# Hybrid backbone on one core: layer norms with centerings first and squares on GpSimd, bias tables two heads at a time

## Chip, cores and metric

The kernel runs on one core of a Trainium2 chip. The metric is the device time of one execution in microseconds (us), the median of the runs. Engines are named as in the profile: PE is TensorE, PEld its weight loads, DVE VectorE, ACT ScalarE, POOL GpSimd, SP the queue of SyncE that issues most of the DMAs.

## What is computed

Two layers over 512 latent and 256 context tokens of width 1024. A layer is a half-step SwiGLU feed-forward network (FFN, inner width 2816), a token mixer, and a second FFN; every sub-layer is modulated by the conditioning vectors and closed by a layer norm.

```python
def layer_norm(x, g, b):
    mu = jnp.mean(xf, axis=-1, keepdims=True)
    var = jnp.mean(jnp.square(xf - mu), axis=-1, keepdims=True)
    return ((xf - mu) * lax.rsqrt(var + LN_EPS)).astype(x.dtype) * g + b

def swiglu(u, w_in, w_out):
    a, v = jnp.split(u @ w_in, 2, axis=-1)
    return (jax.nn.silu(a) * v) @ w_out

def ffn_sublayer(h, shift, scale, gate, w_in, w_out, g, b):
    y = swiglu(modulate(h, shift, scale), w_in, w_out)      # h * (1 + scale) + shift
    return layer_norm(ALPHA * h + FFN_RES * gate * y, g, b)
```

Mixer 0 is a neighbourhood attention (8 x 16 windows on the token grid, 16 heads, a learned bias per head) over latent and context keys; mixer 1 is a windowed attention with grouped keys (band of 128 tokens on each side) over latent and context keys. The shift, scale and gate vectors are products of the conditioning vectors with a large modulation matrix.

## The kernel before

**Layout.** Activations are held transposed: eight tiles `z` of 128 features by all tokens (one of them at times in `zspare`), and their modulated form as a pair of high and low parts, `uh` and `ul`. Weights come as raw tiles `wr` by the SP queue (L94), and are split into `wh` on ACT (L102) and `wl` on POOL (L104), so each product is three matmuls (L153 to L155).

**Stages.** FFN 0a, neighbourhood attention (NA), FFN 0b, FFN 1a, windowed attention (WA), FFN 1b. An FFN runs over chunks 0 to 10 of its inner width and once more over a part of the tokens ("r"). In the middle chunks `seven` (L590) forms two 2x2 block products with seven instead of eight multiplications from sums of token and weight blocks; `sums` and `fourth` (L518 to L559) make the token sums, `fourth` in chunk 1 for the chunks behind. `av` (L465) makes the gated product g as `gh` and `gl` (L478 to L481), and `down` multiplies it by the output weights and adds the result to z on DVE (L453).

**Background products.** `gemv_dve` (L195) computes part of the modulation vectors on DVE while TensorE does an FFN: each product multiplies a tile `wt` (L205, 256 KB by the SP queue) with a broadcast row and sums it into `ga` (L208); the results are then added up and derived into scale and bias of a layer norm (L229, L230, L254 to L262). A pace spreads the products over the chunks; in the last chunks they run thinly, one behind each piece of `av` and `down`.

**Layer norms.** `layer_norm` gives four parts, which are called at points of the program by a table (`plan`, the agenda): `sums` adds the eight z tiles (four on POOL, the rest on DVE), `centers` forms the mean with one matmul and then, tile by tile, subtracts it on DVE (L347), squares on ACT (L419) and adds up the squares (L331), `variance` and `spreading` end in the factor by which `norm` multiplies z (L438). Tiles for squares come from a pool of two (tag "ln"). l0 to l4 are the norms between the stages, `l1_0` that of the first token group behind NA, `l4_0` that of the first group behind WA, `fin_0` and `fin_1` the last ones. `fin_1` sums its squares on TensorE (`layer_norm_pe`).

**Order.** The program is written in one sequence, and the framework's scheduler sets the order of each engine's queue from it; `behind(x, y)` keeps x behind y on one engine. So an edit of the agenda moves rows on all engines.

**Bias tables.** `bias_tables` reads the bias of NA into a scratch tensor `xd` (eight DMAs) and spreads it into `yd`, one DMA of 252 KB for each of 16 heads (L826). NA reads `yd` later into `nb`.

## Time and profile before

| | |
|---|---|
| three timed runs | 2860.63 us median (2854.68, 2860.63, 2862.81) |
| profiled execution | 2868.23 us, span 2866.4 us |
| mean granted clock of PE | 0.972 of full speed |
| busy, PE / PEld | 2728.1 us (95%) / 2447.8 us (85%) |
| busy, DVE / ACT / POOL | 1805.4 us (63%) / 1213.4 us (42%) / 1658.0 us (58%) |
| instructions | 48106 |

A row of a timeline reads: start in us, length in us, engine, line, operation, output <- inputs, shape, count of rows that were merged, and in brackets the idle time of that engine before it and what ended it. PE is busy in 95% of the span, so its waits and its stretches at half clock are what can be read as lost time.

### The profile page before, as it was taken

What the parts mean: (1) busy time and instruction counts of PE and PEld (TensorE: products, weight loads), DVE (VectorE), ACT (ScalarE), POOL (GpSimd) and SP (SyncE); (2) the same over time, 40 slices, a digit from 0 to 9 for tenths busy, and PEclk for the clock granted to TensorE, in tenths of its full rate; (3) what the DMA queues carried; (4) which work ended last, traced back from release to release, by engine and by line L of the source; (5) the groups of instructions that cost most, each with busy time, mean ns of one, the idle gap of its engine ahead of it and who ended that gap; (6) DMA issues with size and microseconds to landing.
All of it is one profiled execution on the core that took longest, in us unless ns stands there. A gap on an engine that the chain in (4) does not pass through costs nothing.

```text
span 2866.4 us, 48106 instructions
## 1 busy us (share of the span) xinstructions
PE 2728.1 (95%) x17122; PEld 2447.8 (85%) x17122; DVE 1805.4 (63%) x4124; ACT 1213.4 (42%) x2497; POOL 1658.0 (58%) x1488
## 2 busy tenths in 40 slices
PE   8999999999999989999999999999998998899997
PEld 5789899888888878999998899998886776888997
DVE  3286777585545676766654776666566667687744
ACT  4223333256454444434333534343246555444443
POOL 4357575375434455876744677765466444577763
PEclk9999999999999989999999999999999999899998
DMA  8525557432212212345462326466522111235562
GB/s 300 141 87 158 133 144 208 134 103 82 60 49 62 58 56 86 97 121 140 119 167 83 96 83 166 134 183 180 174 81 62 31 31 45 59 89 129 123 181 65
DMA packets 286016, 322.42 MB, mean 112 GB/s; under 512 B 28497, under 2 KB 174033, under 8 KB 284753
## 3 DMA queue, kind: packets, MB, share of 16 engines
q1 hardware_dynamic: 269936, 290.89, 34.2%
q0 software_dynamic: 15552, 28.32, 5.9%
q8 instruction: 135, 2.21, 0.3%
q14 instruction: 105, 0.85, 0.1%
q10 hardware_dynamic: 288, 0.14, 0.0%
HBM read 311.41 MB, written 12.25 MB: 113 GB/s over the span
## 4 chain that ended last, share of the span: by engine, by line
PE 52%; DVE 6%; DMA 2%; issue 2%; ACT 1%; POOL 1%; SPq 0%; DVEq 0%; POOLq 0%; ACTq 0%
PE pd1a L153 2%; PE pd0b L153 2%; PE pd1a L154 2%; PE pd0b L154 2%; PE pd0b L155 2%; PE pd1a L155 2%; PE wo L800 1%; PE pd1b L153 1%; PE pd1b L154 1%; PE pd1b L155 1%; DMA wr<-in_wst_dram 1%; PE tpw L791 1%; PE pa1a L153 1%; PE pa1a L154 1%; PE pv1a L153 1%
## 5 line engine op out<-in xcount | busy, mean ns | idle before, releaser
L104 POOL TENSOR_TENSOR wl<-wr,wh 128x512 fp32r<-128x512 f32 x308 | 404.0, 1328 | 298.4 <-ACT wh L102 238.4
L104 POOL TENSOR_TENSOR wl_s<-S,wh_s 128x512 fp32r<-128x512 f32 x202 | 268.4, 1366 | 60.5 <-ACT wh_s L102 59.7
L102 ACT CAST wh<-wr 128x512 fp32r<-128x512 f32 x308 | 186.7, 619 | 215.1 <-DMA wr<-in_wst_dram 62.2
L102 ACT CAST wh_s<-S 128x512 fp32r<-128x512 f32 x216 | 130.9, 620 | 322.4 <-POOL S L574 84.1
L208 DVE CUSTOM_DVE_ANT_0 jk<-wt,cb 128x512 f32<-128x512 f32 x303 | 200.4, 680 | 61.4 <-DMA wt<-in_wmodt_dram 52.1
L574 POOL TENSOR_TENSOR S<-wr,wr 128x512 f32<-128x512 f32 x108 | 146.9, 1360 | 148.6 <-DMA wr<-in_wst_dram 130.1
L104 POOL TENSOR_TENSOR wl_a<-wr,wh_a 128x512 fp32r<-128x512 f32 x120 | 159.1, 1376 | 24.9 <-ACT wh_a L102 24.5
L102 ACT CAST wh_a<-wr 128x512 fp32r<-128x512 f32 x162 | 100.4, 621 | 125.9 <-PE pd1b L154 18.3
L453 DVE SCALAR_TENSOR_TENSOR z<-pd0b,gt,z 128x256 f32<-128x256 f32 (+1 forms) x176 | 103.4, 602 | 62.2 <-PE pd0b L155 62.0
L453 DVE SCALAR_TENSOR_TENSOR z<-pd1a,gt,z 128x512 f32<-128x512 f32 (+1 forms) x168 | 99.8, 619 | 44.5 <-PE pd1a L155 43.3
L807 POOL TENSOR_SCALAR p<-p,l 128x512 f32<-128x512 f32 x64 | 44.6, 698 | 128.9 <-DVE l L906 120.5
L453 DVE SCALAR_TENSOR_TENSOR z<-pd0a,gt,z 128x512 f32<-128x512 f32 (+1 forms) x168 | 98.7, 618 | 29.5 <-PE pd0a L155 28.9
L319 POOL TENSOR_SCALAR z<-z,ag_None,ab_None 128x256 f32<-128x256 f32 (+1 forms) x78 | 63.5, 819 | 53.4 <-DVE uh L305 42.8
L208 DVE CUSTOM_DVE_ANT_0 jk<-zspare,cb 128x512 f32<-128x512 f32 x113 | 75.8, 679 | 15.6 <-DMA zspare<-in_wmodt_dram 15.6
L807 POOL TENSOR_SCALAR pw<-pw,l 128x512 f32<-128x512 f32 (+1 forms) x64 | 41.2, 645 | 74.4 <-DVE l L1097 33.0
L574 POOL TENSOR_TENSOR S<-S,wr 128x512 f32<-128x512 f32 x54 | 77.1, 1427 | 3.2 <-DVE x1b L557 0.7
L574 POOL TENSOR_TENSOR S<-wr,S 128x512 f32<-128x512 f32 x54 | 76.8, 1422 | 2.9
L905 ACT ACTIVATE p<-s,m 128x512 f32<-128x512 f32 x64 | 44.0, 688 | 77.3 <-DVE m L903 72.3
L453 DVE SCALAR_TENSOR_TENSOR z<-pd1b,gt,z 128x512 f32<-128x512 f32 (+1 forms) x98 | 56.8, 609 | 14.8 <-PE pd1b L155 12.3
L306 DVE TENSOR_TENSOR ul<-ufl,uh 128x256 fp32r<-128x256 f32 (+1 forms) x88 | 63.0, 722 | 2.3 <-ACT ufl L301 1.7
L301 ACT ACTIVATE ufl<-z,bi_None,sc_None 128x256 f32<-128x256 f32 (+1 forms) x86 | 54.7, 654 | 22.2 <-DVE z L438 21.9
L153 PE MATMUL pd0a<-gh0a,wh 128*128 128x512 f32 (+1 forms) x144 | 50.6, 365 | 8.3 <-DVE z L453 8.3
(1463 smaller groups left out, 10687.0 us busy)
## 6 DMA issues: line engine op xcount, KB each, us to landing
wr<-in_wst_dram SPq DMA_DIRECT2D x524, 256.0 KB
...
```

What stands on the lines that cost most here:

```text
L102: nc.scalar.copy(hi[:], src[:])
L104: eng.tensor_tensor(out=lo[:], in0=src[:], in1=hi[:].bitcast(F32), op=ALU.subtract)
L153: nc.tensor.matmul(ps, a[0], b[0], start=first, stop=False)
L154: nc.tensor.matmul(ps, a[0], b[1], start=False, stop=False)
L155: last_pe[0] = nc.tensor.matmul(ps, a[1], b[0], start=False, stop=last)
L208: x = nc.vector.tensor_tensor_reduce(out=junk[:], in0=w[:], in1=cb[st], scale=1.0, scalar=0.0, op0=ALU.mult, op1=ALU.add, accum_out=out[st])
L301: nc.scalar.activation(uf[:, :n], zs, AF.Identity, scale=s1, bias=s2)
L306: return hi, nc.vector.tensor_tensor(out=lo, in0=uv, in1=uo.bitcast(F32), op=ALU.subtract)
L319: nc.gpsimd.tensor_scalar(out=zs, in0=zs, scalar1=prm[2][:, d:d + 1], scalar2=prm[3][:, d:d + 1], op0=ALU.mult, op1=ALU.add)
L453: last[0] = nc.vector.scalar_tensor_tensor(out=zt(d, c0, c1), in0=pd, scalar=gt[:, d, st:st + 1], in1=zt(d, c0, c1), op0=ALU.mult, op1=ALU ...
L574: nc.gpsimd.tensor_tensor(out=t[:], in0=a[:], in1=b[:], op=o)
L807: nc.gpsimd.tensor_scalar(out=p, in0=p, scalar1=r, scalar2=0.0, op0=ALU.mult, op1=ALU.add)
```

## The change

1. `layer_norm` now has five parts: sums, mean, centers, variance, spreading. The mean's matmul is a part of its own, and `centers` issues all eight DVE centerings before the first square. For l1_0 and l4_0 (`pool=True`) the eight squares and the seven adds of them run on POOL; ACT loses eight squares for each, DVE five adds and POOL two. The agenda is set anew: for l1_0 the mean stays at o3_0_2 and the centerings move to o3_0_3; for l4_0 sums, mean and centerings are at wo6_2, wo6_3 and wo7_2.
2. The 16 DMAs into `yd` are issued by `bias_rows(2)`, two behind each `seven` of FFN 0a, and no longer in one row after `xd`.
3. `gemv_dve(0)` takes its ranges in the order (40, 72), (24, 40), and the products of 0a end in chunk 9.
4. In `fourth`, and for the weight splits on DVE in FFN 1b, the DVE rows stand behind the last evacuation of g (`evacuated`).
5. `fin_0`'s norm and output are issued inside `layer_norm_pe("fin_1")`, behind fin_1's last centering.

```diff
-    def layer_norm_pe(nm, c0, c1, tags):
+    def layer_norm_pe(nm, c0, c1, tags, between):
...
-        pv = bank(tags[1], f"pv{nm}")
+        pv, made = bank(tags[1], f"pv{nm}"), []
...
-            zs = center(d, c0, c1, pm)
+            zs = center(d, c0, c1, pm, made)
...
+        between(made[-1])
         ve = tp.tile([P, 4], F32, tag="ve", name=f"ve{nm}", bufs=2)[:, :nj]
...
+        def mean():
+            v["pm"] = v["bk"][:, 0:n]
+            behind(nc.tensor.matmul(v["pm"], onesd[:], v["acc"], start=True, stop=True), last_pe[0])
+
         def centers():
-            pm = v["bk"][:, 0:n]
-            behind(nc.tensor.matmul(pm, onesd[:], v["acc"], start=True, stop=True), last_pe[0])
+            zs = [center(d, c0, c1, v["pm"]) for d in range(DT)]
 
             def square(d, acc):
-                zs = center(d, c0, c1, pm)
                 sq = acc if acc is not None else t2(f"sq{nm}_{d}", "ln")[:, :n]
-                nc.scalar.activation(sq, zs, AF.Square)
+                nc.scalar.activation(sq, zs[d], AF.Square)
                 return sq
 
-            v["acc"] = total(f"aq{nm}", n, square, 3, v["part"])
+            if not pool:
+                v["acc"] = total(f"aq{nm}", n, square, 3, v["part"])
+                return
+            v["acc"] = acc = t2(f"aq{nm}")[:, :n]
+            for d in range(DT):
+                sq = t2(f"sq{nm}_{d}", "ln")[:, :n] if d else acc
+                nc.gpsimd.tensor_tensor(out=sq, in0=zs[d], in1=zs[d], op=ALU.mult)
+                if d:
+                    nc.gpsimd.tensor_tensor(out=acc, in0=acc, in1=sq, op=ALU.add)
...
-            nc.vector.tensor_tensor(out=gl[:, c0:c1], in0=pv[:, :n], in1=gh[:, c0:c1].bitcast(F32), op=ALU.subtract)
+            evacuated[0] = nc.vector.tensor_tensor(out=gl[:, c0:c1], in0=pv[:, :n], in1=gh[:, c0:c1].bitcast(F32), op=ALU.subtract)
...
-                nc.vector.tensor_tensor(out=x, in0=x, in1=y, op=ALU.add)
+                behind(nc.vector.tensor_tensor(out=x, in0=x, in1=y, op=ALU.add), evacuated[0])
...
-        weight = [0] + [1.0] * (s0 - 2) + [0] + [1.0] * (NCH - 2 - s0) + [1.2] * (s0 - 1)
+        weight = [0] + [1.0] * (s0 - 2) + [0] + [1.0] * (NCH - 2 - s0) + [1.2]
...
                     seven(f"{nm}_{ci}_{i}", wpos[0] + i, *gs[i])
+                    if mid is not None:
+                        bias_rows(2)
...
-            thin[0] = bool(bg) and NCH - 2 <= (0 if r else ci) < NCH - 3 + s0
+            thin[0] = bool(bg) and ci == NCH - 2
...
-        for h in range(NH):
-            nc.sync.dma_start(yd[h], xd[h].rearrange("r c e -> r (c e)")[:, None, :].broadcast_to([8, 16, RW * 8]))
+
+    heads = list(range(NH))
+
+    def bias_rows(n):
+
+        for _ in range(min(n, len(heads))):
+            h = heads.pop(0)
+            behind(nc.sync.dma_start(yd[h], xd[h].rearrange("r c e -> r (c e)")[:, None, :].broadcast_to([8, 16, RW * 8])),
+                   loaded[0])
...
-            write(layer_norm_pe("fin_1", c0, c1, ("mm", "s", "mm")))
+            write(1, layer_norm_pe("fin_1", c0, c1, ("mm", "s", "mm"), lambda x: write(0, fin[0], x)))
...
-            write(norm)
+            fin.append(norm)
...
-    gemv_dve(0, (24, 40, (0, 1)), (40, 72, (0, 1)))
+    gemv_dve(0, (40, 72, (0, 1)), (24, 40, (0, 1)))
...
-    plan(pon3_0_0_7=l1[0][:1], o3_0_2=l1[0][1:2], pon2_1_256_7=l1[0][2:3], pon2_2_512_7=l1[0][3:4], o3_1_3=l1[0][4:],
...
+    plan(pon3_0_0_7=l1[0][:1], o3_0_2=l1[0][1:2], o3_0_3=l1[0][2:3], pon2_1_256_7=l1[0][3:4], pon2_2_512_7=l1[0][4:5],
...
-    plan(wo6_3=l4[0][:1], wo7_2=l4[0][1:2], pow3_1_256_2=l4[0][2:3], pow3_1_256_6=l4[0][3:5], pow3_1_256_7=l4[1][:1])
+    plan(wo6_2=l4[0][:1], wo6_3=l4[0][1:2], wo7_2=l4[0][2:3], pow3_1_256_2=l4[0][3:4], pow3_1_256_6=l4[0][4:6],
```

**ACT at the end of NA.** These are rows of ACT's queue; p and l are an attention's weights and their row sums, s the scores, tp a transposed p. Before, the squares of l1_0 stand ahead of the exponentials of p of the third key block:

```order
L741 COPY p_0_2_0_10798<-tp_0_2_0_10802 128x512
L419 ACTIVATE aql_0_0_10837<-z_92 128x256
L419 ACTIVATE sql_0_1_10842<-z_93 128x256
L419 ACTIVATE sql_0_2_10846<-z_94 128x256
L419 ACTIVATE pml_0_10767<-z_95 128x256
L419 ACTIVATE sql_0_4_10852<-z_96 128x256
L419 ACTIVATE sql_0_5_10856<-z_97 128x256
L419 ACTIVATE sql_0_6_10860<-z_98 128x256
L419 ACTIVATE sql_0_7_10865<-z_99 128x256
L905 ACTIVATE p_0_3_0_10878,l_0_3_0_10874<-s_0_3_0_10868,m_0_3_0_10873 128x512
L905 ACTIVATE p_0_3_1_10898,l_0_3_1_10894<-s_0_3_1_10888,m_0_3_1_10893 128x512
```

Now, from the same copy on:

```order
L762 COPY p_0_2_0_10795<-tp_0_2_0_10799 128x512
L933 ACTIVATE p_0_3_0_10844,l_0_3_0_10840<-s_0_3_0_10834,m_0_3_0_10839 128x512
L933 ACTIVATE p_0_3_1_10864,l_0_3_1_10860<-s_0_3_1_10854,m_0_3_1_10859 128x512
L762 COPY p_0_3_0_10844<-tp_0_3_0_10848 128x512
L933 ACTIVATE p_1_2_0_11083,l_1_2_0_11079<-s_1_2_0_11073,m_1_2_0_11078 128x512
```

The eight squares are gone from here, and the two exponentials follow the copy.

**POOL at the same place.** L807, and L828 now, is the scaling of p; L885, and L913 now, adds a mask to a bias tile nb. Before:

```order
L885 TENSOR_TENSOR nb_2_11065<-nmask_sb,nb_2_11065 128x768
L331 TENSOR_TENSOR aql_0_0_10837<-aql_0_0_10837,sql_0_1_10842 128x256
L885 TENSOR_TENSOR nb_2_11070<-nmask_sb,nb_2_11070 128x768
L331 TENSOR_TENSOR aql_0_0_10837<-aql_0_0_10837,sql_0_2_10846 128x256
L807 TENSOR_SCALAR p_0_3_0_10878<-p_0_3_0_10878,l_0_3_0_10874 128x512
L807 TENSOR_SCALAR p_0_3_1_10898<-p_0_3_1_10898,l_0_3_1_10894 128x512
```

Now (L438 is the square, L440 the add):

```order
L828 TENSOR_SCALAR p_0_3_0_10844<-p_0_3_0_10844,l_0_3_0_10840 128x512
L828 TENSOR_SCALAR p_0_3_1_10864<-p_0_3_1_10864,l_0_3_1_10860 128x512
L913 TENSOR_TENSOR nb_2_11062<-nmask_sb,nb_2_11062 128x768
L438 TENSOR_TENSOR aql_0_10890<-z_92 128x256
L913 TENSOR_TENSOR nb_2_11067<-nmask_sb,nb_2_11067 128x768
L438 TENSOR_TENSOR sql_0_1_10892<-z_93 128x256
L438 TENSOR_TENSOR sql_0_2_10895<-z_94 128x256
L440 TENSOR_TENSOR aql_0_10890<-aql_0_10890,sql_0_1_10892 128x256
L440 TENSOR_TENSOR aql_0_10890<-aql_0_10890,sql_0_2_10895 128x256
L438 TENSOR_TENSOR sql_0_3_10898<-z_95 128x256
L438 TENSOR_TENSOR sql_0_4_10901<-z_96 128x256
L828 TENSOR_SCALAR p_1_2_0_11083<-p_1_2_0_11083,l_1_2_0_11079 128x512
```

The scaling of p of the third block stands ahead of the squares, that of the next (p_1_2) behind five squares and two adds.

**DVE in chunk 1 of FFN 1b.** L479 and L481 (L497 and L499 now) evacuate g, L453 (L471 now) adds a down product to z, L557 to L559 (L575 to L577) are the fourth sums, L104 a weight split. Before:

```order
L557 TENSOR_TENSOR x1b_4_27764<-x1b_4_27764,x1b_5_27766 128x256
L544 TENSOR_TENSOR T1b_3l<-x1b_1_27318,T1b_3h 128x256
L104 TENSOR_TENSOR wl_a_27805<-wr_00_27796,wh_a_27804 128x512
L557 TENSOR_TENSOR x1b_4_27771<-x1b_4_27771,x1b_5_27773 128x256
L559 TENSOR_TENSOR ul_109<-x1b_4_27764,uh_101 128x2x128
L104 TENSOR_TENSOR wl_a_27809<-wr_01_27798,wh_a_27808 128x512
L479 TENSOR_TENSOR pv1b_1_256_27606<-pv1b_1_256_27606,sl1b_1_256_27631 128x256
L559 TENSOR_TENSOR ul_110<-x1b_4_27771,uh_102 128x2x128
L557 TENSOR_TENSOR x1b_4_27778<-x1b_4_27778,x1b_5_27780 128x256
L453 SCALAR_TENSOR_TENSOR zspare<-pd1b_0_0_27636,gt_8_26702,zspare 128x256
```

Now:

```order
L562 TENSOR_TENSOR T1b_3l<-x1b_2_27316,T1b_3h 128x256
L497 TENSOR_TENSOR pv1b_1_256_27603<-pv1b_1_256_27603,sl1b_1_256_27628 128x256
L471 SCALAR_TENSOR_TENSOR zspare<-pd1b_0_0_27633,gt_8_26699,zspare 128x256
L499 TENSOR_TENSOR gl1b_1_27412<-pv1b_1_256_27603,gh1b_1_27411 128x256
L575 TENSOR_TENSOR x1b_4_27761<-x1b_4_27761,x1b_5_27763 128x256
L575 TENSOR_TENSOR x1b_4_27768<-x1b_4_27768,x1b_5_27770 128x256
L471 SCALAR_TENSOR_TENSOR z_92<-pd1b_0_1_27641,gt_8_26699,z_92 128x256
L575 TENSOR_TENSOR x1b_4_27775<-x1b_4_27775,x1b_5_27777 128x256
L104 TENSOR_TENSOR wl_a_27802<-wr_00_27793,wh_a_27801 128x512
L104 TENSOR_TENSOR wl_a_27806<-wr_01_27795,wh_a_27805 128x512
```

The evacuation of the second half of the tokens and the first add to z stand ahead of the fourth sums and of the weight splits.

## Rows read from the trace of the kernel before

**Rows 1.** The page, its part 1 (busy us, share of the span, instructions of each engine) and, of its part 5, the group of background products on DVE (busy us, mean ns of one | idle of DVE before them, and what ended most of it).

```profile
PE 2728.1 (95%) x17122; PEld 2447.8 (85%) x17122; DVE 1805.4 (63%) x4124; ACT 1213.4 (42%) x2497; POOL 1658.0 (58%) x1488
...
L208 DVE CUSTOM_DVE_ANT_0 jk<-wt,cb 128x512 f32<-128x512 f32 x303 | 200.4, 680 | 61.4 <-DMA wt<-in_wmodt_dram 52.1
```

**Rows 2.** The waits of PE: what waited <- what ended the wait: us in total, times, longest in us.

```profile
PE pd0a L153 <- DVE z L453: 9.0, 5, 6.8
PE pd0a L153 <- DVE gl0a L603: 8.9, 2, 6.9
PE pow L153 <- ACT pw L1084: 8.4, 1, 8.4
PE s L767 <- ACT p L905: 8.4, 1, 8.4
PE pvl L427 <- DVE aql L331: 7.4, 2, 4.1
...
PE pd1b L153 <- DVE zspare L453: 5.8, 2, 5.3
PE pd1a L153 <- DVE gl1a L603: 5.6, 3, 3.8
...
PE pd1b_r L153 <- DVE zspare L453: 2.2, 1, 2.2
```

**Rows 3.** Windows: start:end, length; busy us (instructions) of PE, PEld, DVE, ACT, POOL; granted clock of PE as a share of full speed; busy share of the DMA engines; GB/s. All but the second are the stretch behind a long wait of PE.

```profile
141.88:150.95 9.07, 8.56 (x19) 6.29 (x20) 7.39 (x22) 2.13 (x4) 3.77 (x3) 0.50 0.84 269
...
250.00:300.00 50.00, 46.37 (x264) 43.32 (x263) 34.81 (x86) 18.50 (x34) 31.58 (x27) 1.00 0.56 154
...
318.81:325.03 6.22, 6.21 (x15) 4.86 (x16) 6.22 (x13) 0.07 (x1) 3.15 (x3) 0.50 0.42 126
...
601.10:608.33 7.23, 6.65 (x31) 6.36 (x32) 3.39 (x15) 0.37 (x1) 0.00 (x0) 0.53 0.26 68
...
1018.75:1024.76 6.01, 6.01 (x27) 5.79 (x28) 3.73 (x15) 2.56 (x7) 2.76 (x4) 0.50 0.00 0
...
2435.58:2444.70 9.12, 7.60 (x36) 6.09 (x37) 2.15 (x6) 1.58 (x4) 1.39 (x2) 0.50 0.00 0
...
2534.71:2540.28 5.57, 5.57 (x26) 5.57 (x27) 5.27 (x12) 1.45 (x3) 5.49 (x5) 0.50 0.25 73
```

**Rows 4.** Timelines of the SP queue and of DVE in chunk 1 of FFN 0a.

```profile
116.46 12.21 SPq L826 DMA_DIRECT2D yd<-xd  x14
...
140.13 0.69 DVE L208 CUSTOM_DVE_ANT_0 jk<-wt,cb 128x512 f32<-128x512 f32 x1 [9.65 <-DMA wt<-in_wmodt_dram]
```

**Rows 5.** DVE's instructions of line 260 in the whole run (duration in ns, shortest/median/longest, first and last start in us), then the timelines of DVE and of POOL around the longest of them, and of POOL one chunk later.

```profile
L260 DVE TENSOR_TENSOR bi_None<-sc_None,lnp_sb x5: 160/176/8373, 306.5 to 2073.4; 128x16 f32<-128x16 f32 x5
...
305.80 1.60 POOL L574 TENSOR_TENSOR S<-S,wr 128x512 f32<-128x512 f32 x1
...
306.48 8.37 DVE L260 TENSOR_TENSOR bi_None<-sc_None,lnp_sb 128x16 f32<-128x16 f32 x1
...
312.09 2.73 POOL L104 TENSOR_TENSOR wl_s<-S,wh_s 128x512 fp32r<-128x512 f32 x2
...
414.49 2.82 POOL L104 TENSOR_TENSOR wl_s<-S,wh_s 128x512 fp32r<-128x512 f32 x2
```

**Rows 6.** Timeline of DVE at the end of FFN 0a: the first add of l0_0's sums.

```profile
580.43 1.80 DVE L331 TENSOR_TENSOR ppl<-z,z 128x512 f32<-128x512 f32 x1
```

**Rows 7.** Timelines of ACT and POOL at the end of NA.

```profile
1008.50 1.52 POOL L885 TENSOR_TENSOR nb<-nmask_sb,nb 128x768 f32<-128x768 f32 x1 [3.46 <-DMA nb<-yd]
...
1010.92 0.42 ACT L419 ACTIVATE aql<-z 128x256 f32<-128x256 f32 x1 [4.70 <-DVE z L347]
...
1011.72 0.72 POOL L331 TENSOR_TENSOR aql<-aql,sql 128x256 f32<-128x256 f32 x1 [1.70 <-ACT sql L419]
...
1017.94 0.67 ACT L905 ACTIVATE p<-s,m 128x512 f32<-128x512 f32 x1
```

**Rows 8.** Timelines of DVE, ACT and PE at the end of WA: the last of l4_0's sums, the exponential, the first row of its variance, the first matmul of FFN 1b.

```profile
2418.55 0.42 DVE L331 TENSOR_TENSOR asl<-pml,z 128x256 f32<-128x256 f32 x1
...
2434.77 0.67 ACT L1084 ACTIVATE pw<-sw,m 128x512 f32<-128x512 f32 x1
...
2446.12 0.16 DVE L431 TENSOR_SCALAR pvl<-pvl 128x2 f32<-128x2 f32 x1
...
2452.07 0.55 PE L153 MATMUL pa1b<-uh,wh 128*128 128x256 f32 x1 [2.01 <-DVE uh L305]
```

**Rows 9.** Timeline of DVE in chunk 1 of FFN 1b: two subtractions of the token sums, and the second evacuation of g.

```profile
2514.14 0.41 DVE L544 TENSOR_TENSOR T1b_0l<-x1b,T1b_0h 128x256 fp32r<-128x256 f32 x1
...
2528.05 0.96 DVE L544 TENSOR_TENSOR T1b_3l<-x1b,T1b_3h 128x256 fp32r<-128x256 f32 x1
...
2532.44 0.42 DVE L479 TENSOR_TENSOR pv1b<-pv1b,sl1b 128x256 f32<-128x256 f32 x1
```

**Rows 10.** Timelines of PE and ACT at the end of the program: two matmuls that follow each other, outputs of fin_0, a square of fin_1.

```profile
2831.02 0.28 PE L155 MATMUL pd1b_r<-gh1b_r,wl_0b 128*128 128x256 f32 x1
2831.14 0.28 PE L153 MATMUL pd1b_r<-gh1b_r,wh_0b 128*128 128x256 f32 x1
...
2833.64 3.53 ACT L1225 ACTIVATE ot<-z,lnp_sb 128x256 f32<-128x256 f32 x7
...
2850.29 0.42 ACT L386 ACTIVATE sqfin<-z 128x256 f32<-128x256 f32 x1 [0.44 <-PE pvfin L388]
```

53 lines of the change are left out of this document (31 added, 22 removed).

## The prediction

> **What bounds the kernel now.** I read the busy times first. TensorE is busy 2728.1 of 2866.4 us [rows 1], so only two things can be won: the time in which it waits, and the time in which it runs at half clock. The waits of TensorE by releaser come next [rows 2]: the long ones are few, 4 to 8.4 us each, and each sits at one place. The table of windows [rows 3] then gives, for each such place, the stretch behind the wait in which the granted clock is about 0.50, that is 1.2 instead of 2.4 GHz. Work at half clock costs half of its busy time, so the price of a place is its idle time plus half of the PE busy time in its row. Last I went to each place in the time order of the engine that is waited for [rows 4 to 10].
>
> The profiled execution took 2868.23 us with a span of 2866.4; the three timed runs have a median of 2860.63 (2854.68 to 2862.81). The sum is made against the profiled execution, and its difference is then carried over to the median, 7.6 us lower.
>
> **Bias tables.** The 16 copies xd to yd stand on the SP queue from 116.46 us on, 14 of them in one block of 12.21 us, and a modulation weight (wt) and the next expert weights (wr) are queued behind them. DVE then stands 9.65 us for the wt [rows 4], its next evacuation comes late, and TensorE idles 6.8 us (pd0a for z). Price: 6.8 + 8.56/2 = 11.1. The change issues the copies two at a time in eight calls of `seven`, from about 180 us on. The transfers are not saved: 14 took 12.21 us to issue, so 0.87 each and 1.7 for a pair, in front of that call's later loads. The DMA share in such a stretch is 0.56 [rows 3], and DVE waits on wt already, 52.1 us in all [rows 1]. I take 8 gained; ends 0 (given back in full, as 8 pairs by 1.7 are 14 us of queue time) and 11.
>
> **The bias of layer norm l0 in the middle of 0a.** One DVE instruction on 16 columns, L260, took 8.37 us at 306.48 where the median of its line is 0.176. POOL ran sums and subtractions of weights without a pause from 305.80 on until DVE's row had ended [rows 5]. TensorE idled 6.9 us (pd0a for gl0a): 6.9 + 6.21/2 = 10.0. The change swaps the two ranges of modulation products, so this group comes near 550 us, and the one of layer norm l1, which stood near 586, comes near 417. There POOL is again in such a row, but at its end (414.49 to 417.31), and in the DVE order the last gl evacuation stands ahead of it. I take 7; ends 0 and 10. These rows show DVE held until POOL pauses. The Trainium skill (SBUF — State Buffer, "SBUF: two separate sides") says that DVE and GpSimd arbitrate for a shared port pair, an exclusive lock held for the whole of one instruction. By that rule alone DVE would have been held for one POOL instruction, the term would be near 1 and the sum 34 instead of 40; the measured 8.37 decides, and 7 stays.
>
> **The end of 0a.** All 192 products now finish in chunk 9, so no product and no derived row stands on DVE any more between the last z evacuations and the sums of layer norm l0_0, the first of which starts at 580.43 [rows 6]. Its mean, centerings and variance come some 10 us sooner, and one wait of pvl, 7.4 - 4.1 = 3.3, goes with 6.65/2 behind it: 6.6. Against that, chunks 1 to 9 get 15% more products (193/8.1 = 23.8 instead of 193/9.3 = 20.8 a chunk, each 0.68 [rows 1]): 2.1 us more for DVE in 50, of which 34.8 are busy now [rows 3]. The wt loads come closer by the same ratio; 15% of DVE's 52.1 is 8, and most of that DVE can make up. I take 6 gained less 3 for late wt: 3 (ends -5 and 7).
>
> **l1_0 at the end of neighbourhood attention.** ACT runs eight squares in step with DVE's centerings and adds from 1010.92 on; the exponential that the next scores wait for is queued behind them and starts at 1017.94 [rows 7]. TensorE idles 8.4, with 6.01/2 behind: 11.4. In the change no square of l1_0 stands on ACT, and the exponentials follow the copy of p directly. The mean is formed where it was, the centerings one step later. On POOL, behind the scaling of p3_0_3, there stand now two nb additions (1.52 each) and 15 squares and adds of 128x256. The nearest row for those is POOL's add of that size, 0.72 [rows 7]; a square reads one tile twice, and I take 0.75. The two nb, five squares and two adds, 2 x 1.52 + 7 x 0.75 = 8.3 us, come ahead of the scaling of p3_1_2. TensorE meanwhile has the output projections pon2, 96 matmuls by about 0.12, 11.5 us at full clock (0.28 long in the rows, but started every 0.12 [rows 10]), which cover it if POOL starts in time. I charge 2.4 for a late transposition and take 9 (ends 0 and 11); with the cover gone, all of the 8.3 would be paid.
>
> **l4_0 at the end of window attention.** The same picture: the exponential starts at 2434.77 [rows 8], behind eight squares, TensorE idle 8.4, then 7.60 busy at half clock: 12.2. Here the new chain is on the path, since 1b can begin only with l4_0's norm. The sums end at 2418.97 and the mean no longer waits behind the next outputs, so the centerings can start near 2422. POOL then needs 15 by 0.75 and three other instructions between them at some 0.9, 14 us, to about 2436; the steps from the variance (2446.12 now) to the first matmul of 1b (2452.07) took 6 us. First matmul near 2443 against 2452.07, the half clock behind it partly kept: I take 8 (ends -4 and 12).
>
> **Fourth sums.** In 1b, DVE has sums and weight subtractions ahead of the second evacuation of chunk 1, which runs only at 2532.44 [rows 9]; TensorE idles 5.3 (pd1b for zspare) and then runs 5.57 at half clock: 8.1. These rows now stand behind the last gl. Late next is the last ul of the fourth sums, by some 3 us; nothing on TensorE asks for it before the next chunk. In 0a, 0b and 1a the same edit moves adds that no wait of rows 2 names: nothing there, the downs of chunk 1 cover it. I take 6 (ends 0 and 8).
>
> **Centerings first elsewhere.** At l3_1, at the start of WA, pvl waits 4.1 us [rows 2]. There the first squares are added up on POOL, behind two wl subtractions; this stays, and only the taking of turns between ACT and DVE behind it shortens. I take half: 2 (ends 0 and 4).
>
> **The end.** fin_0's eight norms leave DVE from before the last evacuations, so the wait of 2.2 (pd1b_r for zspare) goes. In exchange, ACT has four outputs of fin_0, 0.5 each, ahead of the last two squares of fin_1, partly in gaps of 0.44 [rows 10]: some 1.3 us on the path. Eight more output transfers start near 2855, just before the last ones. I take 1 gained (ends -5 and 2).
>
> **The sum.** 8 + 7 + 3 + 9 + 8 + 6 + 2 + 1 = 44. I charge 4 for waits that the new order makes at places that nothing here shows, one wait of the size of pd1a for gl1a (3.8 [rows 2]). So 40: 2828.2 for a profiled execution, and **2820.6** against the median.
>
> **Rivals.** (1) The stalls come back elsewhere in 0a: the pairs of copies cost what their block did, DVE is held near 417 as it was at 306, and wt comes late. For it: POOL's row at 414.49 and DVE's 52.1 us on wt. Against: gl stands ahead in the order. The first three terms, 18, go: 2838.6. Chance 0.17. (2) POOL becomes the bound at the two ends of attention. A DVE subtraction of two SBUF tiles took 0.96 beside POOL and 0.41 alone [rows 9]; if POOL's 15 pay as much, 0.55 each, a block grows by 8 us, and at each of the two places 8 of the gain go: 2836.6. Against: the DVE rows that stand beside these blocks read PSUM for the most part. Chance 0.12. The Trainium skill (Perfetto Trace Analysis, "Optimizing Scalar/DVE Operations") says of work moved between DVE and GpSimd that it "might not help", since they share a port, which speaks against this change; the 0.96 agrees. (3) Slower: the copies hold up each `seven` in which they stand. Each time that wr and wt come as late as at 135 us, 11.1 are lost; with 36 gained elsewhere (without the first term, before the charge of 4) it turns at the fourth of the eight calls, five give 2884 and all eight 2917. For it: the same queue, the same bytes. Against: a pair is a seventh of the block of 14. Chance 0.05. (4) The waits change their names but not their length, since other waits of the same chains end just behind: within 8 us of now, 2856. Chance 0.08.
>
> **How the numbers follow.** The forecast has 0.58. A measurement of this kernel can tell about 0.3%, 8.6 us, from no change. The forecast and rivals 1 and 2 are faster, 0.87; same 0.07, nearly all rival 4; slower 0.06, rival 3 and a rest. The ends of the terms, which will not all fall on one side, put the forecast between 2800 and 2834; rivals 1 and 2 with half of their bounds reach 2848. The range is 2800 to 2848.
>
> **What would show it.** Right: no wait of TensorE above 6 us at the downs of chunk 1 in 0a, at its sevens, or at s and pow for the exponentials; POOL's squares at 0.72 to 0.8 each; a mean clock of 0.98 or more; no wait of pd1b for zspare above 2. Wrong: wr landing late behind yd; POOL's squares above 1.2; waits of tp for POOL's p or of pvl for POOL's aql above 5 us; a tail behind the last matmul longer than now.

## The result, and the profile after

The change takes 2819.36 us (median of 4 runs, 2817.81 to 2822.0) beside 2861.72 of the kernel before (4 runs, 2854.68 to 2866.77): ratio 0.9854, 95% interval 0.9834 to 0.9873. The forecast was 2820.6. In a later set, together with two experiments, the same kernel gave 2822.56 beside 2858.0: 0.9881 (0.9860 to 0.9902). The profiled execution took 2817.81 us with a span of 2816.0. A difference of some 5 us between two kernels is therefore not read as one below, unless a row of the trace shows its place.

The mean granted clock is 0.988 where it was 0.972. Part 1 of the page and the group of background products, which answer to [rows 1]:

```profile
PE 2704.6 (96%) x17122; PEld 2426.0 (86%) x17122; DVE 1788.5 (64%) x4114; ACT 1207.1 (43%) x2481; POOL 1673.5 (59%) x1514
...
L210 DVE CUSTOM_DVE_ANT_0 jk<-wt,cb 128x512 f32<-128x512 f32 x297 | 196.9, 681 | 54.5 <-DMA wt<-in_wmodt_dram 50.8 <-ACT cb L227 3.4
```

TensorE does the same 17122 matmuls in 23.5 us less busy time, because less of it lies at half clock, and idles less. The waits of PE by releaser, which answer to [rows 2]:

```profile
PE pd0a L155 <- DVE gl0a L622: 10.9, 5, 3.7
...
PE pd1b L155 <- DVE gl1b L622: 5.4, 3, 3.4
...
PE pd1a L155 <- DVE gl1a L622: 3.8, 3, 2.2
...
PE tp L812 <- POOL p L828: 2.8, 2, 2.0
PE pd0a L155 <- DVE z L471: 2.5, 6, 0.8
...
PE pvl L445 <- DVE aql L333: 1.7, 1, 1.7
```

The five waits above 5 us of [rows 2] are gone; but for the first loads of the program, no wait is above 4 any more. What has grown is pd1b for gl1b (2.7 before) and pd0a for gl0a (8.9 before), the latter by three waits of 2.4 to 3.7 in the sevens of 0a. The table of windows at the first place of [rows 3], same columns, shows full clock:

```profile
131.05:140.12 9.07, 8.66 (x42) 6.83 (x41) 7.83 (x23) 2.00 (x4) 4.27 (x4) 1.00 0.88 275
```

The first of l0_0's sums stands at 566.92 instead of 580.43 [rows 6], the second evacuation of chunk 1 in 1b at 2479.31 instead of 2532.44 [rows 9], the first matmul of 1b at 2407.64 instead of 2452.07 [rows 8]:

```profile
566.92 0.70 DVE L333 TENSOR_TENSOR ppl<-z,z 128x512 f32<-128x512 f32 x1
```

```profile
2479.31 0.42 DVE L497 TENSOR_TENSOR pv1b<-pv1b,sl1b 128x256 f32<-128x256 f32 x1
```

```profile
2407.64 0.55 PE L155 MATMUL pa1b<-uh,wh 128*128 128x256 f32 x1 [2.04 <-DVE uh L307]
```

Where the time came from, in profiled executions: the length of each stage in us, from the first matmul of its first tile to that of the next stage (pd0a, pq, pa0b, pa1a, vw, pa1b, end of the span). The experiments are described below.

| kernel | up to pd0a | 0a | NA | 0b | 1a | WA | 1b to end | span |
|---|---|---|---|---|---|---|---|---|
| before | 74.7 | 536.5 | 432.9 | 549.8 | 540.3 | 317.9 | 414.3 | 2866.4 |
| change | 73.0 | 526.5 | 422.1 | 541.8 | 537.1 | 307.1 | 408.4 | 2816.0 |
| change again | 73.1 | 526.2 | 422.1 | 544.3 | 538.5 | 307.4 | 407.9 | 2819.5 |
| copies in one block | 75.5 | 527.3 | 421.3 | 541.5 | 536.4 | 307.5 | 408.5 | 2818.0 |
| copies late | 72.7 | 533.0 | 424.7 | 545.4 | 537.2 | 307.7 | 410.8 | 2831.5 |
| old order, old pace | 71.8 | 523.6 | 424.4 | 544.0 | 534.8 | 307.1 | 408.0 | 2813.7 |
| old order, new pace | 72.3 | 517.3 | 421.2 | 545.0 | 539.8 | 307.6 | 407.2 | 2810.4 |
| new order, old pace | 73.1 | 523.9 | 424.9 | 544.0 | 539.5 | 308.4 | 412.2 | 2826.0 |
| no squares on POOL | 72.8 | 523.1 | 418.1 | 547.1 | 543.2 | 307.3 | 411.4 | 2823.0 |
| centerings in turns | 72.8 | 531.0 | 426.4 | 547.0 | 544.9 | 309.2 | 411.4 | 2842.7 |
| in turns at l1 only | 73.0 | 526.9 | 422.4 | 545.7 | 535.5 | 308.0 | 411.2 | 2822.7 |
| before + centerings first | 75.8 | 534.4 | 425.9 | 544.8 | 534.9 | 313.9 | 411.2 | 2840.9 |
| fourth sums as before | 73.7 | 527.7 | 421.7 | 543.8 | 543.8 | 307.6 | 414.0 | 2832.3 |
| fin_0 as before | 70.7 | 524.5 | 420.9 | 541.5 | 541.1 | 309.6 | 410.2 | 2818.5 |

The two executions of the change show how far one stage differs by itself: 2.5 us in 0b, 1.4 in 1a, under 0.6 elsewhere. The five kernels whose edit touches only 0a (the copies, the order, the pace) spread more: 541.5 to 545.4 in 0b, 534.8 to 539.8 in 1a, 407.2 to 412.2 in 1b. So where a stage differs by less than that, the place is looked for by comparing the start of the same matmul in two executions. Every stage of the change is shorter than before, and 0b and 1a by 8.0 and 3.2, where the prediction had named nothing; the 3.2 of 1a are within this spread.

### The profile page after: what moved, and what is told of

It reads as the page before. It is cut to its first block, busy times and chain, and to the rows that moved or that the text cites. A ratio compares the mean times of both kernels' runs of the same rounds, so it can differ in the third digit from the quotient of the medians.

```text
span 2816.0 us, 48073 instructions
## 1 busy us (share of the span) xinstructions
PE 2704.6 (96%) x17122; PEld 2426.0 (86%) x17122; DVE 1788.5 (64%) x4114; ACT 1207.1 (43%) x2481; POOL 1673.5 (59%) x1514
## 4 chain that ended last, share of the span: by engine, by line
PE 50%; DVE 8%; DMA 3%; ACT 2%; issue 2%; POOL 1%; SPq 0%; DVEq 0%; ACTq 0%; POOLq 0%
PE pd0b L155 2%; PE pd0b L156 2%; PE pd0b L157 2%; DMA wr<-in_wst_dram 2%; PE pd1a L155 2%; PE pd1a L156 2%; PE pd1a L157 2%; PE wo L821 1%; PE pd1b L155 1%; PE pd1b L156 1%; PE pd1b L157 1%; DVE z L471 1%; PE tpw L812 1%; PE pa1a L156 1%; DMA wt<-in_wmodt_dram 1%
## 5 line engine op out<-in xcount | busy, mean ns | idle before, releaser
L104 POOL TENSOR_TENSOR wl<-wr,wh 128x512 fp32r<-128x512 f32 x308 | 405.1, 1331 | 277.4 <-ACT wh L102 213.8
L104 POOL TENSOR_TENSOR wl_s<-S,wh_s 128x512 fp32r<-128x512 f32 x202 | 269.0, 1365 | 48.1 <-ACT wh_s L102 36.6
L104 POOL TENSOR_TENSOR wl_a<-wr,wh_a 128x512 fp32r<-128x512 f32 x120 | 158.5, 1363 | 20.0 <-ACT wh_a L102 13.9
L471 DVE SCALAR_TENSOR_TENSOR z<-pd0b,gt,z 128x256 f32<-128x256 f32 (+1 forms) x176 | 103.1, 603 | 58.2 <-PE pd0b L157 58.0
L471 DVE SCALAR_TENSOR_TENSOR z<-pd1a,gt,z 128x512 f32<-128x512 f32 (+1 forms) x168 | 99.5, 621 | 44.2 <-PE pd1a L157 40.3
L471 DVE SCALAR_TENSOR_TENSOR z<-pd0a,gt,z 128x512 f32<-128x512 f32 (+1 forms) x168 | 98.6, 621 | 34.2 <-PE pd0a L157 33.7
L828 POOL TENSOR_SCALAR p<-p,l 128x512 f32<-128x512 f32 x64 | 44.5, 697 | 119.4 <-DVE l L934 114.7
L321 POOL TENSOR_SCALAR z<-z,ag_None,ab_None 128x256 f32<-128x256 f32 (+1 forms) x78 | 62.1, 800 | 47.0 <-DVE uh L307 33.3
L828 POOL TENSOR_SCALAR pw<-pw,l 128x512 f32<-128x512 f32 (+1 forms) x64 | 41.2, 644 | 67.2 <-DVE l L1125 21.0
L471 DVE SCALAR_TENSOR_TENSOR z<-pd1b,gt,z 128x512 f32<-128x512 f32 (+1 forms) x98 | 56.6, 610 | 14.7 <-PE pd1b L157 14.3
L155 PE MATMUL vn<-wh,uh 128*128 128x256 f32 x192 | 54.8, 286 | 1.0 <-DVE nq L775 0.6
```

The lines of the kernel that those rows point to most:

```text
L104: x = eng.tensor_tensor(out=lo[:], in0=src[:], in1=hi[:].bitcast(F32), op=ALU.subtract)
L155: nc.tensor.matmul(ps, a[0], b[0], start=first, stop=False)
L321: nc.gpsimd.tensor_scalar(out=zs, in0=zs, scalar1=prm[2][:, d:d + 1], scalar2=prm[3][:, d:d + 1], op0=ALU.mult, op1=ALU.add)
L471: last[0] = nc.vector.scalar_tensor_tensor(out=zt(d, c0, c1), in0=pd, scalar=gt[:, d, st:st + 1], in1=zt(d, c0, c1), op0=ALU.mult, op1=ALU ...
L828: nc.gpsimd.tensor_scalar(out=p, in0=p, scalar1=r, scalar2=0.0, op0=ALU.mult, op1=ALU.add)
```

## The experiments

Each undoes one part of the change; one does a single part alone in the kernel before. The ratios are to the kernel before, measured with it on the same chip.

### The copies of the bias tables: one block, or all late

```diff
             behind(nc.sync.dma_start(xd[:, r], ...), loaded[0])
+        bias_rows(16)
```

> The changed kernel, but with all 16 copies xd to yd in one block behind xd, as before. Theory A (the block costs 11 us at 135 us, and the pairs give a part of that back in the sevens): the wait of pd0a for z near 135 us is there again with 6 to 7 us, DVE's waits on wt in the sevens shrink; in sum 3 to 8 us slower than the changed kernel, 2822 to 2827. Rival B (the pairs give all of it back): within 2 us of the changed kernel's 2819.4. Rival C (the pairs cost nothing): 11 us slower, 2830.

Measured: 2824.33, ratio 0.9884 (0.9866 to 0.9901): the time lies in theory A's span, but the ratio, beside 0.9854 and 0.9881 for the change, doesn't tell A from rival B. The second of the pair puts all 16 behind the last `seven` of 0a:

```diff
-                    if mid is not None:
-                        bias_rows(2)
+                    if mid is not None and ci == NCH - 3 and i == 1:
+                        bias_rows(16)
```

> The changed kernel, but with all 16 copies xd to yd issued behind the last seven of FFN 0a, so none in chunks 3 to 6 and none at 116 us. Theory A (the pairs hold up the loads of wr and wt in the sevens): PE's waits of pd0a for gl0a between 240 and 310 us (3.7 and 2.4 us) go, and the kernel is 4 to 8 us faster than the changed one, 2811 to 2815, unless the late block stops chunk 10. Rival B (wt is late because 15% more products are asked for per chunk, whatever else is on the queue): those waits stay and the time is within 2 us of 2819.4.

Measured: 2836.77, ratio 0.9929 (0.9913 to 0.9945), slower than either expectation had it. The waits of PE with the block, and its DVE row behind the block:

```profile
PE pd0a L155 <- DVE z L471: 12.4, 7, 7.1
...
PE pd0a L155 <- DVE gl0a L622: 5.3, 3, 3.6
```

```profile
141.26 0.69 DVE L210 CUSTOM_DVE_ANT_0 jk<-wt,cb 128x512 f32<-128x512 f32 x1 [9.94 <-DMA wt<-in_wmodt_dram]
```

The block brings the wait of [rows 4] back, 9.94 on DVE and 7.1 on TensorE. But in the sevens, gl0a is waited for 5.3 us instead of 10.9, and 0a is as long as in the change (527.3 to 526.5 and 526.2). So in this kernel, with the other edits in it, the loss moves from chunk 1 to the sevens: rival B, by the stage. In the change a pair stands for 1.36 us on the SP queue ahead of the next wt loads, and DVE waits 5.70 us for wt soon after:

```profile
238.72 1.36 SPq L853 DMA_DIRECT2D yd<-xd  x2
```

```profile
246.16 0.69 DVE L210 CUSTOM_DVE_ANT_0 jk<-wt,cb 128x512 f32<-128x512 f32 x1 [5.70 <-DMA wt<-in_wmodt_dram]
```

The pairs aren't the only reason: with all copies late this wait is 5.5, and DVE waits for wt as long in all (the rows below are of 150 to 600 us in that run; in the change it is 30.6). Yet something of the sevens' loss is theirs. TensorE's wait at 305.7 is gone with the copies late, and at the same matmul that run is ahead of the change by 4.0 us at 320 and by 5.0 at 440. By 480 it is 5.9 behind. Its copies stand on the SP queue from 431 to 454, six and three of them in one row, DVE waits 10.6 us at once for the row cb, the conditioning vector of the next range (4.8 in the change), and TensorE idles 8.46 at 478.58, where it idles 3.4 in the change.

```profile
DVE jk L210 <- DMA wt<-in_wmodt_dram: 31.2, 11, 5.5
...
DVE jk L210 <- ACT cb L227: 13.2, 2, 10.6
```

So the 7 us in 0a have their place. The 2 to 4 us more in several later stages were not explained by any row that I found; they stay open.

### The order of the ranges, and the pace of the products

Three kernels: the ranges and the pace as before; the ranges alone as before; the pace alone as before.

```diff
-    ... gemv_dve(0, (40, 72, (0, 1)), (24, 40, (0, 1)))
+    ... gemv_dve(0, (24, 40, (0, 1)), (40, 72, (0, 1)))
```

```diff
-        weight = [0] + [1.0] * (s0 - 2) + [0] + [1.0] * (NCH - 2 - s0) + [1.2]
+        weight = [0] + [1.0] * (s0 - 2) + [0] + [1.0] * (NCH - 2 - s0) + [1.2] * (s0 - 1)
...
-            thin[0] = bool(bg) and ci == NCH - 2
+            thin[0] = bool(bg) and NCH - 2 <= (0 if r else ci) < NCH - 3 + s0
...
-                if thin[0]:
+                if thin[0] and ci == NCH - 4 + s0:
```

> The changed kernel, but with the background products of FFN 0a as before: ranges (24, 40) then (40, 72), the pace of before, the last products in chunk 10. Theory A: DVE's row for the bias of l0 near 306 us is held for some 8 us again and PE waits 5 to 7 us behind it; at the end of 0a the norms l0 begin 10 us later again; the sevens behind chunk 4 win 6 to 8 us back: 8 to 14 us slower than the changed kernel, 2827 to 2833. Rival B (the denser products cost as much as the free end of 0a gives): within 3 us of 2819.4.

Measured: 2815.49, ratio 0.9854 (0.9836 to 0.9873).

> The changed kernel, but with the two ranges of background products in the order of before, (24, 40) then (40, 72), at the pace of the change. Theory A (DVE instructions on small tiles wait as long as POOL's run of instructions on SBUF tiles goes on): L262, the bias of l0, falls near 300 us into such a run again, takes 3 us or more there, and the kernel is 4 to 10 us slower than the changed one, 2823 to 2829. Rival B (8.37 us was an accident of one run, and one POOL instruction is the most that DVE waits): L262 takes under 1.7 us and the time is within 2 us of 2819.4.

Measured: 2818.03, ratio 0.9860 (0.9842 to 0.9878).

> The modulation products keep the change's order of the two ranges, but come at the pace of the kernel before: 20.8 a chunk instead of 23.8, the rest in the last two chunks of 0a. Theory: the sevens of 0a gave back some 11 us because 15% more products a chunk bring the weights wt too late; at the old pace DVE waits for wt about 14 us instead of 31, the waits of pd0a for gl0a near 250 and 478 shrink, and against that pvl waits 3.4 us again for the squares of l0 at the end of 0a: 0a shorter by 3 to 9 us, the whole 2 to 8 us shorter than the change. Rival A: the waits of the sevens come from the pairs of bias copies; they stay, and with the wait at the end of 0a the time is 0 to 5 us longer than the change. Rival B: the bias of a layer norm is held again next to POOL's row, as in the run with the old order and the old pace; then the same as the change.

Measured: 2823.56, ratio 0.9876 (0.9855 to 0.9896). None differs from the change by its time; for the first two that is rival B. The row that was held for 8.37 us [rows 5], L262 now (all five instructions of the line; shortest/median/longest ns), in the change, with the old order and pace, and with the old order alone:

```profile
L262 DVE TENSOR_TENSOR bi_None<-sc_None,lnp_sb x5: 157/175/176, 409.2 to 2039.6; 128x16 f32<-128x16 f32 x5
```

```profile
L262 DVE TENSOR_TENSOR bi_None<-sc_None,lnp_sb x5: 164/175/5912, 294.0 to 2037.4; 128x16 f32<-128x16 f32 x5
```

```profile
L262 DVE TENSOR_TENSOR bi_None<-sc_None,lnp_sb x5: 158/175/221, 276.9 to 2035.1; 128x16 f32<-128x16 f32 x5
```

With order and pace of before the hold is back (5.91 us), and so is a wait of 5.9 of pd0a for gl0a; yet 0a is 2.9 us shorter than in the change, since the waits that the change has in its later sevens are not there. The old order alone has no hold either, so the order of the ranges is not what frees DVE: the moment is, against POOL's row. With the old pace alone, TensorE is ahead of the change of the same set, at the same matmul, by 7.3 us at 400, by 10.0 from 500 to 550, and by 0.6 at 610: nearly all it gains in the sevens it loses at the end of 0a, where the last products stand ahead of l0's sums again. DVE's waits for wt from 150 to 600 us are 15.1 in it, and 25.7 in the change of the same set. Its waits of PE:

```profile
PE pvl L445 <- DVE aql L333: 5.0, 2, 3.4
PE pd0a L155 <- DVE gl0a L622: 4.3, 3, 2.9
```

My expectation of 2 to 8 us less was wrong; of it, only the smaller waits in the sevens came true.

It isn't the pace alone that costs in the sevens. The old order at the new pace is ahead of the change by 6.0 us at 350 and by 9.9 at 500, and keeps all of it at the end of 0a: it has the shortest 0a of all, 517.3. DVE waits for wt there as long as in the change of the later set (26.3). What differs at the later place is the row cb. In the change it is due in a seven, first row below, and TensorE idles 3.4 behind it at 482.1; all nine executions with the new order and the new pace have that wait, of 3.1 to 8.5. With the old order at the new pace (the other two rows: DVE from 150 to 600 us, and PE) cb is due at 400.8, the wait for it is 2.7, and TensorE idles 1.6 soon after:

```profile
477.16 0.69 DVE L210 CUSTOM_DVE_ANT_0 jk<-zspare,cb 128x512 f32<-128x512 f32 x1 [4.81 <-ACT cb L227]
```

```profile
DVE jk L210 <- ACT cb L227: 3.3, 2, 2.7
```

```profile
PE pd0a L155 <- DVE gl0a L622: 6.4, 3, 3.6
```

So the loss in the sevens came with the swap of the ranges at the new pace; some 4 of the 9.9 us lie at cb, and the 6 by 350 lie near 250 and 300, where no single row names them. This is one execution, the fastest of four (2812.16 beside 2817.62 to 2822.33), and the times don't show it.

### The squares of l1_0 and l4_0 back from POOL

```diff
-    l1 = [ln(..., held=False, pool=i == 0) for i, g in enumerate(g3)]
+    l1 = [ln(..., held=False) for i, g in enumerate(g3)]
...
-    l4 = [ln(..., ("mm", "o")[i], pool=i == 0) for i, g in enumerate(g1)]
+    l4 = [ln(..., ("mm", "o")[i]) for i, g in enumerate(g1)]
```

> The squares and adds of l1_0 and l4_0 stand on ACT and DVE again instead of POOL; everything else is as in the change (mean apart, all centerings first, order of the steps). Theory: TensorE waited there because the exponential stood on ACT behind the squares. At the end of NA the squares now stand between the exponentials of p3_0_3 and those of p3_1_2, so a part of the wait of s for p comes back, 2 to 6 us with half of the work behind it; at the end of WA the exponential of pw7_3 stands behind all eight squares again, a wait of pow for pw of 6 to 9 us with 7.6 busy at half clock behind it, against a variance that is ready some us sooner. Sum: 5 to 14 us longer than the change, 2824 to 2833. Rival: that the mean is apart and the centerings stand first is what gained, POOL is not needed: within 2.5 us of the change, and no wait of pow for pw above 3.

Measured: 2821.92, ratio 0.9872 (0.9858 to 0.9885): the rival. TensorE waits for no exponential of these two places again. ACT at the end of WA in this run:

```profile
2388.71 0.42 ACT L429 ACTIVATE aql<-zspare 128x256 f32<-128x256 f32 x1
...
2392.84 0.95 ACT L429 ACTIVATE sql<-z 128x256 f32<-128x256 f32 x2
...
2394.25 0.69 ACT L1112 ACTIVATE pw<-sw,m 128x512 f32<-128x512 f32 x1
```

The eight squares take 5.1 us here; in the kernel before the first of them started at 2427.64, 7.1 us ahead of the exponential of [rows 8]. It still stands behind them, but TensorE no longer waits for it. On POOL the same sum takes longer than on ACT and DVE. The end of NA, first the change (eight centerings, first row of the variance), then without POOL:

```profile
994.07 2.74 DVE L349 TENSOR_TENSOR z<-z,pml 128x256 f32<-128x256 f32 x8 [1.22 <-PE pml L422]
...
1013.01 0.17 DVE L449 TENSOR_SCALAR pvl<-pvl 128x2 f32<-128x2 f32 x1
```

```profile
991.09 2.73 DVE L349 TENSOR_TENSOR z<-z,pml 128x256 f32<-128x256 f32 x8 [1.22 <-PE pml L422]
...
1002.14 0.16 DVE L449 TENSOR_SCALAR pvl<-pvl 128x2 f32<-128x2 f32 x1
```

18.9 us from centerings to variance with POOL, 11.1 without. NA is 4.0 shorter without, and 0b longer by 2.8 to 5.3; over both nothing is left. The Trainium skill (Perfetto Trace Analysis, "Optimizing Scalar/DVE Operations") says of work moved between DVE and GpSimd that it "might not help"; here it neither helped nor hurt.

### All centerings first: taken out of the change, and alone in the kernel before

```diff
-            zs = [center(d, c0, c1, v["pm"]) for d in range(DT)]
+            zs = [center(d, c0, c1, v["pm"]) if pool else None for d in range(DT)]
...
-                nc.scalar.activation(sq, zs[d], AF.Square)
+                nc.scalar.activation(sq, center(d, c0, c1, v["pm"]), AF.Square)
```

> In the layer norms that don't use POOL, centering and square alternate per block as in the kernel before; the mean stays apart, and l1_0 and l4_0 keep POOL. Theory: the gain of 4 to 5 us at l1_1 and l1_2 (the start of 0b) and of about 2 at l3_1 comes from the centerings that stand first, since the squares of ACT then no longer wait for each of them: 4 to 8 us longer than the change, the loss at the starts of 0b and WA, and pvl waits 4 us at l3_1 again. Rival: those gains follow from what became early ahead of them (POOL's part, the mean apart); then within 2 us of the change.

Measured: 2841.4, ratio 0.9938 (0.9925 to 0.9950), 16 to 24 us more than the change and three times the expectation. At the same matmul of the change's second execution, some 10 of the 23 us between the two lie where layer norms stand (the start of NA, from the end of NA to chunk 1 of 0b, and the start of WA), and some 13 in sevens of 0a, 1a and 1b, where no layer norm stands and other kernels differ too. So the time overstates what the turns cost. The next kernel does the same in l1_1 and l1_2 alone (`if pool or not nm.startswith("l1")`):

> Centering and square in turns only in l1_1 and l1_2, at the end of neighbourhood attention and the start of 0b; everything else as in the change. Theory: the largest part of what in_turns lost is here, because there the centerings, the squares of ACT, the sums of squares and the evacuations of 0b's chunk 0 share DVE and ACT: 5 to 9 us longer than the change, all between the last output projections and chunk 1 of 0b. Rival: the loss is spread evenly over all such layer norms, or came from the sevens of 0a and 1a, whose waits differ from one execution to the next: 0 to 3 us.

Measured: 2826.37, ratio 0.9888 (0.9869 to 0.9907), beside 0.9881 for the change in the same set. At the same matmul of the change of this set it is 1.0 us behind at 1020, 5.8 at 1080, and 2.5 from 1200 on, so 1.5 us come here: the rival's size, so l1 is not where most of it lies. The last kernel is the one before with this one edit:

```diff
+            zs = [center(d, c0, c1, pm) for d in range(DT)]
             def square(d, acc):
-                zs = center(d, c0, c1, pm)
                 sq = acc if acc is not None else t2(f"sq{nm}_{d}", "ln")[:, :n]
-                nc.scalar.activation(sq, zs, AF.Square)
+                nc.scalar.activation(sq, zs[d], AF.Square)
```

> The kernel before, with one edit: all eight centerings of a layer norm stand ahead of its squares; the mean is formed where it was, nothing is on POOL, everything else as before. Theory, from the run that took this edit out of the change and lost some 15 to 20 us: the edit is worth as much by itself, 10 to 20 us faster than before (2838 to 2848 beside 2858), with the gain at the end of neighbourhood attention, the starts of 0b, 1a, WA and 1b, where the squares of ACT no longer wait for DVE. Rival A, the prediction's price: it helps at l3_1 and little elsewhere, 0 to 4 us. Rival B: it works only together with the mean apart, because without it eight centerings stand in a row ahead of DVE's evacuations: within 3 us or slower, with new waits of pd0b or pd1a for z.

Measured: 2839.96 beside 2861.24, ratio 0.9927 (0.9901 to 0.9954): 13 to 28 us faster, half of what the whole change gives, as the theory had it. By the table of stages it is 2.1 in 0a, 7.0 in NA, 5.0, 5.4, 4.0 and 3.1 in the rest. At the same matmul, some 19 us lie where layer norms stand: 2.1 at the start of NA, 9.7 from its end to chunk 1 of 0b, 2.5 at the start of WA, 5.0 from its end to chunk 1 of 1b. The 2.1 of 0a and the 5.4 of 1a lie in sevens, and the start of 1a gains nothing, against the theory.

TensorE idles 12.7 us less and is busy 12.8 less (2715.3), as its mean clock rises from 0.972 to 0.978. Of its waits, prl for yl, a late step of a layer norm, nearly goes, and sw for pw (scores in WA) halves to 2.7. They stood in the list of the kernel before, between the lines that [rows 2] shows, and then here:

```profile
PE prl L370 <- DVE yl L342: 6.7, 5, 2.4
...
PE sw L1060 <- ACT pw L1084: 5.1, 4, 3.0
```

```profile
PE prl L370 <- DVE yl L342: 0.9, 1, 0.9
```

Where the time was lost is seen from ACT. Its waits ahead of a square that is not a layer norm's first (us, times, longest), in the kernel before, with the one edit, in the change, and in the change with turns:

```profile
ACT sql L419 <- DVE z L347: 25.2, 22, 2.3
```

```profile
ACT sql L420 <- DVE z L347: 0.6, 2, 0.3
```

```profile
ACT sql L429 <- DVE z L349: 0.9, 3, 0.3
```

```profile
ACT sql L429 <- DVE z L349: 17.4, 16, 2.3
```

25.2 us in 22 waits, each below 2.4, lie on the chain from a mean to its variance; they go with the edit (other waits of ACT ahead of squares grow by some 6 us) and come back with turns. Not all of them are paid for: 4.2 us stand at the start of 1a, where TensorE gains nothing. One such chain at the start of 0b: DVE's centerings and the last addition of the squares, before and in the change.

```profile
1059.26 1.40 DVE L347 TENSOR_TENSOR z<-z,pml 128x256 f32<-128x256 f32 x4
...
1062.25 0.42 DVE L347 TENSOR_TENSOR z<-z,pml 128x256 f32<-128x256 f32 x1 [1.25 <-ACT pml L419]
...
1071.19 0.41 DVE L331 TENSOR_TENSOR aql<-pml,sql 128x256 f32<-128x256 f32 x1
```

```profile
1038.00 2.73 DVE L349 TENSOR_TENSOR z<-z,pml 128x256 f32<-128x256 f32 x8
...
1043.58 0.42 DVE L333 TENSOR_TENSOR aql<-pml,sql 128x256 f32<-128x256 f32 x1
```

12.3 us became 6.0. In turns a centering queues on DVE behind evacuations, the square waits for it, the addition for the square, and the next centering for a free tile. With the one edit, the waits of s for p (8.4 to 5.7) and of pow for pw (8.4 to 5.4) shrink too, as the squares ahead of the exponentials go faster, but they stay:

```profile
PE s L768 <- ACT p L906: 5.7, 1, 5.7
PE pow L153 <- ACT pw L1085: 5.4, 1, 5.4
```

In the run without POOL they are gone; what it has and this one lacks is, at those places, the mean as a part of its own and the new agenda.

### The fourth sums, and fin_0, where they were

```diff
-                behind(nc.vector.tensor_tensor(out=x, in0=x, in1=y, op=ALU.add), evacuated[0])
+                nc.vector.tensor_tensor(out=x, in0=x, in1=y, op=ALU.add)
...
-            if eng is nc.vector:
-                behind(x, y)
```

> The fourth sums and the subtractions of token sums stand on DVE where they stood in the kernel before, not behind the last evacuation. Theory: in 1b DVE has them ahead of the second evacuation of chunk 1 again, TensorE waits 5.3 us (pd1b for zspare) and runs about 5.6 at half clock; against that the wait of pd1b for gl1b at 2530.78 in the change (3.4) does not come. Net 1 to 6 us longer than the change, all of it between the first matmul of 1b and its chunk 3; 0a, 0b and 1a as in the change. Rival A: the wait only moved, net within 1 us. Rival B: in 0a, 0b or 1a too the adds ahead of an evacuation cost, over 8 us in all.

Measured: 2830.05, ratio 0.9897 (0.9878 to 0.9915). The wait is back, and the second evacuation (second row) stands behind the subtractions again; its place in the change, 2479.31, would be 2490.3 here, as 1b's first down is 11.0 us later:

```profile
PE pd1b L153 <- DVE zspare L469: 5.0, 2, 4.5
```

```profile
2494.89 0.42 DVE L495 TENSOR_TENSOR pv1b<-pv1b,sl1b 128x256 f32<-128x256 f32 x1
```

From the first matmul of 1b to the end it is 5.6 to 6.1 longer than the change, but only in part where the theory had it. Counted from the first matmul of 1b, the next sevens (p01b) start at 90.2, where the change has 87.4 and 86.9; the sevens after those start at 132.3, where the change has 132.4 and 129.8, since its wait of pd1b for gl1b just ahead of them (3.4 and 2.9) is 1.5 here. So by then 0 to 2.5 us are left, near rival A, and the rest comes in later sevens, where kernels without this edit differ as much. Of the 5 to 7 us more in 1a, 1.4 are there by its first sevens; the rest comes in later ones, and runs of other kernels have it too (543.2 without POOL).

```diff
-            fin.append(norm)
+            write(0, norm)
```

> fin_0 is normalised and written where it was in the kernel before, ahead of the last evacuations, not between the steps of fin_1. Theory: the wait of pd1b_r for zspare (2.2 us, with half of the work behind it at half clock) comes back, and the tail behind the last matmul stays at 11.0: 2 to 4 us longer than the change. Rival: the tail gets shorter by the outputs that stand in it, 1 to 2 us, and the time is within 1.5 us of the change.

Measured: 2826.4, ratio 0.9884 (0.9865 to 0.9903), the runs between 2817 and 2832. The wait of pd1b_r for zspare returns (1.9), the tail behind the last matmul is 11.0 in both, and the stage is 1.8 to 2.3 longer, of which 0.9 lie between the first matmul of pd1b_r and the end: the theory's direction, below its size; the times can't tell it.

### The change once more

> The changed kernel itself, for a figure beside the runs of the same chip: 2815 to 2825, a ratio of 0.985 to 0.987 to the kernel before.

Measured: 2822.56 (5 runs, 2821.25 to 2832.87), ratio 0.9881, the time inside the expected span, the ratio just above it.

## Why the prediction was right in its sum, and wrong in half of its steps

The predicted gain was 40 us; 42 were measured in the first set and 35 in the later one, 50.4 between the two profiled executions. That it fits is partly luck: terms that came to little and one that was ten times too small made up for each other.

**Bias tables (8), l0's bias (7), end of 0a (3).** Together 18; the stage gained 10.0. Each wait that was named went: 6.8, 6.9 and 3.3. But the gains don't add up. With the pairs (and the edits outside the products) 0a is 12.9 us shorter than in the kernel before, with the new pace as well 19.2, and with the swapped ranges on top only 10.0; there the pairs win 1 us over the block. Each is one execution. The step that failed is the swap, priced at 7: at the new pace the row that was held for 8.37 us is not held with the old order either (0.22 at most), and the swap costs 9.2 in these executions. The sum has no term for the row cb, for which DVE now waits 4.8 us in a seven; that is some 4 of the 9.2, and the cause of the rest stays open. Beside that, the end of 0a was worth more than the 6 of its term: the two runs with the old pace lose 8 to 10 us there. And late wt, "8, and most of that DVE can make up", 3 in the sum, met a loss of 10 in the sevens, which either the old order or the old pace takes away. The first rival is right that the sevens lose (with the copies late they lose 5 less up to 440) and has half of the size; DVE was not held near 417.

**l1_0 (9) and l4_0 (8).** NA gained 10.8 and WA 10.8, so the sizes fit. The cause did not: of these, 7.0 and 4.0 come with the centerings alone, nothing with POOL, some 1.5 at the start of NA with the new pace (both runs with the old pace lose it there), and the rest, by exclusion, with the mean apart and the new agenda, which no run tried alone. The step that failed is "here the new chain is on the path" with POOL's squares as its remedy; the chain on POOL takes 18.9 us against 11.1 without. The rival of POOL as the bound was right that its chain is slow, and wrong in its price: the longest wait of tp for POOL's p is 2.0, as before, and NA's 4.0 come back in 0b.

**Fourth sums (6).** The wait went as described, and the whole stage fits (5.6 to 6.1), by luck: two groups of sevens later 0 to 2.5 us of it are left, since TensorE then waits for gl1b, and what the stage shows beyond that comes in sevens that differ without this edit too.

**Centerings first elsewhere (2).** The largest error: 21 by itself (13 to 28), some 19 of it where layer norms stand; taken out, some 10 there. The step took only those waits of TensorE that bear the name of a square's sum, one of 4.1 at l3_1. It passed over prl for yl, 6.7, and sw for pw, 5.1, and took s and pow to go only with the squares, though both shrink by some 3 us when the squares merely go faster. The waits ahead of all these stood on ACT, 25.2 us in 22 pieces, and half of what came back in the profile is TensorE's busy time, as less of it lies at half clock.

**The end (1).** Right in size: 0.9 from the first matmul of pd1b_r on; not to be told from nothing by the times.

**The charge for new waits (4).** One came as described: pd1b for gl1b 3.4, and three in 0a.

The third rival's sum mixes two counts: 2884 and 2917 have the charge of 4 in them, and with it the sum turns at the third call (33.3 against 32), not at the fourth. That rival did not come.
